# An attention stage issued in the order of a list plan, with wider products and four gates moved to the dense stage, in a one-core hybrid encoder block

## The chip, the cores and the metric

The kernel runs on 1 core of a Trainium2 chip. The core has five engines, each with its own queue of instructions: PE (TensorE, matrix products, with its weight loads listed apart as PEld), DVE (VectorE), ACT (ScalarE), POOL (GpSimd) and SP (SyncE, which here only issues transfers). [...] The metric is the device time of one execution in microseconds (us), lower is better.

## The reference

One layer of a streaming encoder, for 1024 frames of width 1024, in float32. A normed input goes through one combined projection, whose columns feed three token mixers and three gates. The mixers are a gated linear recurrence (HGRN, 4 heads of 128), forgetting attention (FoX, 8 heads of 64) and cross-attention into 256 memory tokens (4 heads of 128). Each mixer's result is projected, multiplied by its gate, and the sum is projected and added to the input; a convolutional GLU of width 2816 follows.

```python
h = _rmsnorm(x, norm_mix_g[l])
z = h @ w_in[l]
(hq, hf, hi, hg, fq, fk, fv, ff, mq, gate_logits) = jnp.split(z, pts, axis=-1)
y_a = _hgrn2_mixer(hq, hf, hi, hg, lower_bounds[l], hgrn_norm_g[l])
y_b = _fox_mixer(fq, fk, fv, ff, fox_f_bias[l], fox_q_norm_g[l], fox_k_norm_g[l])
...
y_c = _memory_mixer(mq, mem_kv, mem_q_norm_g[l], mem_k_norm_g[l])
gates = jax.nn.sigmoid(gate_logits).reshape(B, T, N_BRANCH, D_MODEL)
merged = (gates[:, :, 0] * (y_a @ w_br_hgrn[l]) + gates[:, :, 1] * (y_b @ w_br_fox[l])
          + gates[:, :, 2] * (y_c @ w_br_mem[l]))
x = x + merged @ w_out[l]
x = x + _conv_glu_ffn(_rmsnorm(x, norm_ffn_g[l]), ...)
```

The part that the change is about is FoX. For a block of 128 queries and all keys up to its end, per head:

```python
s = (jnp.einsum('bhqd,bhkd->bhqk', qh[:, :, lo:hi], kh[:, :, :hi]) * scale
     + Fc[:, :, lo:hi, None] - Fc[:, :, None, :hi])
p = jax.nn.softmax(jnp.where(mask, s, -jnp.inf), axis=-1)
outs.append(jnp.einsum('bhqk,bhkd->bhqd', p, vh[:, :, :hi]))
```

## The kernel before

**Number format.** A float32 operand is split (`split`, L172) into a high part, cast on ACT, and a low part, subtracted on DVE. One product block is then three matmuls, high by high, high by low and low by high (`mm3`, L158, lines L160 to L162 in the profile). Products go into four kinds of PSUM bank: `pp` (three), `lg` and `tr` (two each), `po` (one).

**Stages.** The kernel issues, in this order: the load and split of the input with the first gates; the *dense stage*, where pairs of 128-column chunks are projected at once by a fast scheme with seven block products in place of eight (`dense_unit`, L628, over `PAIRS`; the chunks are the four of the memory queries and `NPAIR` = 10 gates); the *memory stage* with cross-attention, beside the FoX values and the first q/k projection (L974); the *attention stage* (L980 to L985 and L1229 to L1235); the HGRN heads; the branches and the output projection; the feed-forward part, where both projections use the seven-product scheme again.

**Gates.** There are 24 chunks of gates. A gate that is not in the dense stage is projected alone by `gates_early` (L470) through `cm_chunk` (L200): for each half of the frames, eight `mm3` of 512 columns; DVE multiplies by the norm (L464), ACT applies tanh (L465) and SP sends the result to DRAM (`gd`), from where the branches fetch it. Ten of them are given to the attention stage, by `NFOX` = [0, 3, 0, 3, 0, 3, 1].

**Token-major projections.** `token_major` (L704) computes eight blocks of 128 frames by `ncol` channels, eight `mm3` each. `fox_proj(p)` (L844) makes q and k of head pair p, 256 columns, evacuated by ACT (L853) and normed (L859 to L862, with a POOL power at L179). `hgrn_values` (L1012) makes the HGRN values in two pieces of 256 columns, written straight into `Vf` over the FoX values. `fox_prep` (L866) transposes a pair's q and k by PE and splits them for the two heads on ACT, DVE and POOL.

**Attention.** `fox_attn(p, i)` (L901) works on one head. For each of eight query blocks, `rows`: scores in pieces of up to 512 keys (L924, L925), decay and running maximum by DVE (L930), exponent by ACT (L940), reciprocal by DVE (L941), normalising by POOL (L942). After each two blocks: transposes of the weights (L953, L954, L956), split by ACT and DVE, products with the values for 256 queries (L965, L966), and the sum of high and low parts (L969, L970) to DRAM (`ybd`).

**Order.** Python generators are woven together by `weave` (L97): a head's attention, at raised priority, with a token-major projection or with gates. The order of the instructions on each engine is then chosen by the framework's own scheduler, from these priorities and a model of time; `tc.issue_after` adds single edges. Weight blocks wait in three pairs of buffers, `wh` and `wl`.

```python
    for p in range(3):
        weave((ahead(fox_attn(p, 0), AHEAD), FOX_STEPS), (fox_proj(p + 1), 8))
        fox_prep(p + 1, fox_sets[p][3])
        weave((ahead(fox_attn(p, 1), AHEAD), FOX_STEPS), (gates_early(NFOX[2 * p + 1]), 2 * NFOX[2 * p + 1], FOX_LATE))
```

**After the attention.** `hgrn_prep(0)` projects the first HGRN head (six blocks, L1043). Before the memory branch its operands come back from DRAM by POOL transfers, all issued behind the last HGRN norm. In the feed-forward part `unit` (L1452) runs one seven-product unit; for the first of them `families` (L1495) makes the operand blocks, with two of the low parts of `B21` on POOL, and `spread` (L361) makes the norm's row.

Of the kernel before, what the change touches and what calls it, by code (L numbers as in the profile page):

```python
# [28 lines left out]
NCOVER, NPAIR = 2, 10  # L29
NDULL = 8  # L30
NFOX = [0, 3, 0, 3, 0, 3, 1]
# [3 lines left out]
assert 2 + NCOVER + NPAIR + sum(NFOX) == len(ORDER) and len(_dense) % 2 == 0  # L35
# [3 lines left out]
FOX_STEPS, HGRN_STEPS, MEM_STEPS = 28, 14, 7  # L39
AHEAD = 300  # L40
FOX_LATE = 0.2
# [66 lines left out]

@with_exitstack
def tile_block(ctx: ExitStack, tc: tile.TileContext, xT, memT, x_rows, mem_rows, vec, fbias, mats, hmask, w_first, w_cm, w_hi, w_fqk, w_fv,  # L110
# [77 lines left out]
    def weights(src, shape, raw=None, hl=None, parts=1):  # L188
# [4 lines left out]
        if hl is None:  # L193
            hl = [wp.tile([P, 4 * 264], F32R, tag=t, name=t, bufs=3) for t in ("wh", "wl")]
# [166 lines left out]
    def spread(r, rcol):  # L361

        for n in range(2):
            ps = ps_tr()
# [57 lines left out]
    def first_weights(k):  # L422
        k0, k1 = WFIRST[k]
        if k % 4 == 0:
            gw[k // 4] = [wp.tile([P, 4 * 264], F32R, tag=t, name=t, bufs=3) for t in ("wh", "wl")]
        sl = slice((k0 % 4) * 256, (k1 - 1) % 4 * 256 + 256)
        split(S, gw[k // 4][0][:, sl], gw[k // 4][1][:, sl], wg[k // 4][:, sl])
# [124 lines left out]
    def product(ps, op, b, first):  # L552
        wh, wl = op
        for k in range(4):
            ks = slice(k * P, (k + 1) * P)
            bh, bl = block(b, k)
            mm3(ps, wh[:, ks], wl[:, ks], bh, bl, first and k == 0, k == 3, not first)

    class Dense:
# [16 lines left out]
        def operand(self, src):  # L576
            if self.half is None:
                self.half = [wp.tile([P, 4 * 264], F32R, tag=t, name=t, bufs=3) for t in ("wh", "wl")]
# [125 lines left out]
    def token_major(src, ncol, evac):  # L704

        with tc.issue_after(late["load"].ins):
            w = [weights(src[q], (4, ncol)) for q in range(2)]
        for tb in range(8):
            ps = ps_proj()[:, :ncol]
            tsl = slice(tb * P, (tb + 1) * P)  # L710
            for k in range(KC):
                wh, wl = w[k // 4]
                mm3(ps, uh[k][:, tsl], ul[k][:, tsl], wh[:, k % 4, :], wl[:, k % 4, :], k == 0, k == KC - 1)
# [127 lines left out]
    fox_sets = {}  # L841
    fox_z = {}

    def fox_proj(p):  # L844

        fox_z[p] = [None, None]

        def evac(tb, ps):
            n, b = tb // 4, tb % 4
            if b == 0:  # L850
                fox_z[p][n] = pq.tile([P, 4, 256], F32, tag="z", name=f"z{p}_{n}", bufs=2)
            z = fox_z[p][n]
            S.activation(z[:, b, :], ps, AF.Copy, scale=rt[:, tb:tb + 1])  # L853
            if b == 3:
                zz = z.rearrange("p b (h d) -> p (b h) d", d=64)
                sq = pools["pf"].tile([P, 16, 64], F32, tag="pt", name="fsq", bufs=4) if p else \
                    pm.tile([P, 16, 64], F32, tag="fsq", name="fsq")
                r = cp.tile([P, 16], F32, tag="fr", name="fr", bufs=2)
                S.activation(sq, zz, AF.Square)  # L859
                V.reduce_sum(r, sq, axis=AX.X)  # L860
                rstd_small(r, r, 64)
                V.tensor_mul(zz, zz, r.unsqueeze(2).to_broadcast([P, 16, 64]))  # L862

        yield from token_major(w_fqk[p], 256, evac)

    def fox_prep(p, after=None):  # L866
        kh = [pf.tile([P, T], F32R, tag=f"kh{i}", name=f"kh{i}_{p}", bufs=1 + i) for i in range(2)]
        qa = [pf.tile([P, T], F32R, tag=f"qa{i}", name=f"qa{i}_{p}", bufs=1 + i) for i in range(2)]
        kl = [pf.tile([P, T], F32R, tag=f"kl{i}", name=f"kl{i}_{p}", bufs=1 + i) for i in range(2)]
        for n in range(2):  # L870
            sl = slice(n * HB, (n + 1) * HB)
            z = fox_z[p][n]
            for what in range(2):
                gc = col(C_FK) if what == 0 else fqs
                ptr = ps_tr()
                with tc.issue_after(after.ins) if after is not None else nullcontext():
                    for b in range(4):
                        PE.transpose(ptr[:, b * P:(b + 1) * P], z[:, b, what * P:(what + 1) * P], ident)
                for i in range(2):
# [935 lines left out]
```

## Time and profile before

| what | us |
|---|---|
| median of 3 runs | 1698.56 |
| lowest and highest run | 1698.53 and 1700.1 |
| the profiled execution, its own time | 1700.23 |
| its span, first to last instruction | 1698.4 |

The profile was taken from one execution, at a mean granted clock of PE of 0.999. In the lists of groups, a row gives the line, engine and operation, the tile written and those read, the shape and the count; then the busy time of the group and the mean duration of one; then the idle time of the engine in front of them and what ended it. In a table of stretches, each engine has its busy time and, behind x, the instructions that touch the stretch. The duration printed for a matmul is longer than the time until the next one starts, since they are pipelined; the pace of PE is read from starts or from counts. A transfer's row gives its queue, the count, the size and the median time from issue to landing.

### The profile page before, as it was taken

Reading aid. Unit: us, or ns where it says so; the run is one execution under the profiler, and the core shown is the slowest. Engines: PE = TensorE matmul, PEld = TensorE weight load, DVE = VectorE, ACT = ScalarE, POOL = GpSimd, SP = SyncE. Lnnn points to the kernel's source line nnn. Section 1 sums busy time; section 2 is a strip of 40 time slices with the busy share of each in tenths; the row PEclk is TensorE's granted clock in tenths of the full one; section 3 lists DMA queues with packets and bytes.
Section 4 is the critical chain, followed back from the end, with each engine's and each line's share of the span. In section 5 each row is a group of like instructions: output and inputs, shape, how many; then the busy total and the mean of one; then the engine's idle time right before and its main releaser. Section 6 shows DMA issues by size and latency. Waiting matters only on the chain.

```text
span 1698.4 us, 24291 instructions
## 1 busy us (share of the span) xinstructions
PE 1691.0 (100%) x8957; PEld 1452.4 (86%) x8957; DVE 1150.8 (68%) x2057; ACT 800.9 (47%) x1428; POOL 324.6 (19%) x420
## 2 busy tenths in 40 slices
PE   9999999999999999999999999999999999999999
PEld 7888899989898998888888888888888888888887
DVE  6966455666666664886856845987878888775654
ACT  6734455545454553775631333644434444533432
POOL 0200032543433331544310000311111111100000
PEclk9999999999999999999999999999999999999999
DMA  9443232221212111110346542566544344494772
GB/s 367 157 161 106 88 139 68 77 92 51 94 59 77 63 46 57 67 32 13 106 127 209 167 186 100 165 174 169 158 139 138 118 149 143 172 363 145 251 269 87
DMA packets 83062, 227.16 MB, mean 134 GB/s; under 512 B 9712, under 2 KB 12408, under 8 KB 82816
## 3 DMA queue, kind: packets, MB, share of 16 engines
q1 hardware_dynamic: 64320, 160.54, 26.8%
q0 software_dynamic: 18048, 64.50, 13.2%
q8 instruction: 70, 1.15, 0.3%
q10 hardware_dynamic: 576, 0.59, 0.1%
q14 instruction: 48, 0.39, 0.1%
HBM read 180.72 MB, written 67.93 MB: 146 GB/s over the span
## 4 chain that ended last, share of the span: by engine, by line
PE 99%; DVE 0%; ACT 0%; DMA 0%; issue 0%; ACTq 0%; DVEq 0%
PE pp L160 21%; PE pp L162 21%; PE pp L161 21%; PE lg L160 4%; PE lg L162 4%; PE lg L161 4%; PE tr L162 3%; PE tr L161 3%; PE tr L160 3%; PE po L966 1%; PE lg L925 1%; PE lg L924 1%; PE po L965 1%; PE po L160 1%; PE po L161 1%; PE po L162 1%
## 5 line engine op out<-in xcount | busy, mean ns | idle before, releaser
L160 PE MATMUL pp<-uh,wh 128*128 128x512 f32 x412 | 163.3, 396 | 0.0
L161 PE MATMUL pp<-ul,wh 128*128 128x512 f32 x412 | 162.9, 395 | 0.0
L162 PE MATMUL pp<-uh,wl 128*128 128x512 f32 x412 | 162.5, 394 | 0.0
L161 PE MATMUL pp<-wl,uh 128*128 128x256 f32 (+1 forms) x512 | 146.3, 286 | 0.0
L162 PE MATMUL pp<-wh,ul 128*128 128x256 f32 (+1 forms) x512 | 146.1, 286 | 0.0
L160 PE MATMUL pp<-wh,uh 128*128 128x256 f32 (+1 forms) x512 | 145.6, 286 | 0.0
L166 ACT CAST wh<-s 128x512 fp32r<-128x512 f32 x110 | 66.5, 621 | 131.6 <-PE pp L161 55.1
L166 ACT CAST wh<-raw 128x1024 fp32r<-128x1024 f32 (+2 forms) x76 | 67.6, 890 | 100.6 <-PE pp L161 86.2
L166 ACT CAST wh<-rw 128x512 fp32r<-128x512 f32 x87 | 53.2, 619 | 108.1 <-PE pp L161 70.2
L160 PEld LDWEIGHTS pp<-wh,uh 128*128 128x128 f32 x512 | 97.3, 190 | 1.2
L161 PEld LDWEIGHTS pp<-wl,uh 128*128 128x128 f32 x512 | 97.4, 190 | 1.0
L162 PEld LDWEIGHTS pp<-wh,ul 128*128 128x128 f32 x512 | 97.4, 190 | 0.9
L1457 POOL DMA_DIRECT2D rw<-in_w_up x44 | 24.1, 555 | 372.4 <-DVE wl L1350 171.3
L166 ACT CAST dwh<-wr 128x1024 fp32r<-128x1024 f32 (+1 forms) x41 | 40.2, 980 | 115.8 <-PE tr L161 40.0
L162 PEld LDWEIGHTS pp<-uh,wl 128*128 128x128 f32 x412 | 77.5, 188 | 15.1
L174 DVE TENSOR_TENSOR wl<-raw,wh 128x1024 fp32r<-128x1024 f32 (+2 forms) x75 | 78.0, 1040 | 17.8 <-ACT wh L166 17.6
L160 PEld LDWEIGHTS pp<-uh,wh 128*128 128x128 f32 x412 | 77.5, 188 | 14.6
L161 PEld LDWEIGHTS pp<-ul,wh 128*128 128x128 f32 x412 | 77.5, 188 | 14.5
L940 ACT ACTIVATE pt<-pt,st 128x128 f32<-128x128 f32 (+3 forms) x64 | 49.7, 777 | 41.7 <-DVE st L937 33.9
L174 DVE TENSOR_TENSOR dwl<-wr,dwh 128x1024 fp32r<-128x1024 f32 (+1 forms) x41 | 46.3, 1129 | 31.7 <-ACT dwh L166 31.7
L942 POOL TENSOR_SCALAR pt<-pt,st 128x128 f32<-128x128 f32 (+3 forms) x64 | 49.1, 767 | 78.4 <-DVE st L941 64.1
L1350 DVE TENSOR_TENSOR wl<-rw,wh 128x512 fp32r<-128x512 f32 x69 | 47.7, 704 | 22.7 <-PE pp L162 18.2
(500 smaller groups left out, 5123.2 us busy)
## 6 DMA issues: line engine op xcount, KB each, us to landing
rw<-in_w_up POOLq DMA_DIRECT2D x44, 512.0 KB, 4.7
sd<-in_w_dn POOLq DMA_DIRECT2D x30, 512.0 KB, 6.0
br<-yd SPq DMA_DIRECT2D x30, 512.0 KB, 5.0
raw<-in_w_cm SPq DMA_DIRECT2D x24, 512.0 KB, 3.4
gd<-gt SPq DMA_DIRECT2D x48, 256.0 KB, 2.0
gt<-gd SPq DMA_DIRECT2D x48, 256.0 KB, 2.7
yd<-fc SPq DMA_DIRECT2D x44, 256.0 KB, 2.2
wr<-sd SPq DMA_DIRECT2D x20, 512.0 KB, 4.5
```

What stands on the lines that cost most here:

```text
L160: PE.matmul(ps, lh, rh, start=first, stop=False, skip_group_check=more)
L161: PE.matmul(ps, lh, rl, start=False, stop=False, skip_group_check=more)
L162: return PE.matmul(ps, ll, rh, start=False, stop=last, skip_group_check=more)
L166: return S.copy(out, in_)
L174: return (sub or V).tensor_sub(l, src, h.bitcast(F32))
L924: PE.matmul(ps[:, :w], qa[i][:, tsl], kh[i][:, s0:s0 + w], start=True, stop=False)
L925: fox_sets[p][3] = PE.matmul(ps[:, :w], qa[i][:, tsl], kl[i][:, s0:s0 + w], start=False, stop=True)
L940: S.activation(pt[:, :ns], pt[:, :ns], AF.Exp, bias=st[:, 2:3], accum_out=st[:, 3:4])
L942: G.tensor_scalar(pt[:, :ns], pt[:, :ns], st[:, 3:4], 0.0, ALU.mult, ALU.add)
L965: PE.matmul(o, vhl[:, sb, :], ph[:, src], start=(sb == 0), stop=False)
L1350: late["split"] = V.tensor_sub(l, src, h.bitcast(F32))
L1457: late["raw"] = G.dma_start(raw[:, 2 * i:2 * i + 2, :], src[:, 2 * i:2 * i + 2, :])
```

## The change

Attention, its projections and its filler become *chains*: generators that yield an engine, a cost, and the earliest start, before they trace each instruction. `Plan.run` repeatedly takes the chain whose next step can start first (the lower rank at a tie), advances that engine's time and traces the step. `Plan.pin` adds to every instruction an order edge, without a semaphore, behind the one traced before it on its engine; so on all engines the order is that of the plan. `Ring` keeps the turn of rotating buffers. The costs are linear formulas. Steps of attention on PE get `SLACK` = 0.8 us on top of the time at which their inputs are ready.

Ranks: the chains of split and product after each transpose or score group 0, transposes of a head's weights 1, scores, values and decay rows 2, the pairs' q and k 3 (their evacuation 2), the later pairs' norm 4, weights 5, values back 6, filler 9. The filler, in order: the 256-column projection of pair 1; q and k of pairs 2 and 3 in one product of 512 columns (`w_late[0]`), sent to DRAM and fetched back per pair; six gates; the HGRN values in one product of 512 columns (`w_late[1]`), sent to DRAM and fetched into `Vf` when the last head's values are split. A head's weights are transposed and multiplied in two groups of four query blocks (512 queries).

Beside that: `NPAIR` is 14 in place of 10, so four gates move to the dense stage; `wh` and `wl` have four buffers; the first weights of HGRN are staged within the plan; the memory branch's operands are fetched two at a time behind gate loads of the first branch; in the opening of the feed-forward part a few steps change place or engine; and the store for POOL's transfer descriptors is set to 2048 bytes.

```diff
-NCOVER, NPAIR = 2, 10
+NCOVER, NPAIR = 2, 14
 NDULL = 8
...
-NFOX = [0, 3, 0, 3, 0, 3, 1]
+NFOX = 6
...
+SLACK = 0.8
+WIDE = 4
...
+    def pin(self):
+        traced = self.bb.bb.instructions
+        for i in traced[self.seen:]:
+            e = str(i.engine)
+            if e in self.last:
+                self.tc.add_manual_dep(i, self.last[e].name, mybir.DependencyInfo(
+                    mybir.DependencyClass.NoSync, mybir.DependencyReason.DATA), reason="order of the plan")
+            self.last[e] = i
+        self.seen = len(traced)
+
+    def run(self):
+        while self.chains:
+            self.chains.sort(key=lambda c: c[0])
+            for c in list(self.chains):
+                if callable(c[2]):
+                    t = c[2]()
+                    if t is not None:
+                        self.step(c, t)
+                        break
+            else:
+                best = min((c for c in self.chains if not callable(c[2])),
+                           key=lambda c: (max(c[2][2], self.free.get(c[2][0], 0.0)), c[0]))
+                eng, cost, ready = best[2]
+                start = max(ready, self.free.get(eng, 0.0))
+                self.free[eng] = start + cost
+                self.step(best, start)
...
+def pe_us(n):
+    return max(0.109, n * 0.000446)
+
+def act_us(n):
+    return 0.1 + 0.00082 * n
+
+def exp_us(n):
+    return 0.29 + 0.00084 * n
+
+def dve_us(n):
+    return 0.07 + 0.00105 * n
+
+def pool_us(n):
+    return 0.28 + 0.00083 * n
+
+
+PE_LAG, LAG = 0.25, 0.12
+LOAD, STORE = 4.0, 3.0
...
+    def rows():
+        for h in range(8):
+            p, i = divmod(h, 2)
+            t0 = yield lambda: max(qk_ready[p]) if len(qk_ready.get(p, ())) == 8 else None
...
+                    k, t = yield from lg.get()
                     ps = ps_lg()
-                    PE.matmul(ps[:, :w], qa[i][:, tsl], kh[i][:, s0:s0 + w], start=True, stop=False)
-                    fox_sets[p][3] = PE.matmul(ps[:, :w], qa[i][:, tsl], kl[i][:, s0:s0 + w], start=False, stop=True)
...
+                    t = yield "PE", 2 * pe_us(w), max(t, t0) + SLACK
+                    PE.matmul(ps[:, :w], qa[:, tsl], kh[:, s0:s0 + w], start=True, stop=False)
+                    PE.matmul(ps[:, :w], qa[:, tsl], kl[:, s0:s0 + w], start=False, stop=True)
+                    t += 2 * pe_us(w) + PE_LAG
+                    plan.add(0, reduced(row, s0, w, ps, k, max(t, tp, ts), nfm, kf, tf))
+            rows_done[h] = t
...
+    def outcomes():
+        for h in range(8):
+            tv = yield lambda: vh_ready.get(h)
+            for g in range(2):
+                pts = []
+                t0 = tv
+                for tb in range(4 * g, 4 * g + 4):
+                    yield lambda: (h, tb) in pt_ready or None
+                    pts.append(pt_ready[h, tb][0])
+                    t0 = max(t0, pt_ready[h, tb][1])
+                for sb in range(4 * g + 4):
+                    k, t = yield from tr.get()
+                    ptr = ps_tr()
+                    first = max(sb - 4 * g, 0)
+                    t = yield "PE", (4 - first) * pe_us(P), max(t, t0) + SLACK
+                    for j in range(first, 4):
+                        PE.transpose(ptr[:, j * P:(j + 1) * P], pts[j][:, sb * P:(sb + 1) * P], ident)
+                    t += (4 - first) * pe_us(P) + PE_LAG
+                    plan.add(0, outcome(h, g, sb, first, k, ptr, t))
+                pt_free[h, g] = t
+
+    def outcome(h, g, sb, first, k, ptr, t):
+        c = slice(first * P, HB)
+        w = HB - first * P
+        kp, tp = yield from pls.get()
+        ph = pf.tile([P, HB], F32R, tag="ph", name="ph", bufs=2)
+        pl = pf.tile([P, HB], F32R, tag="pl", name="pl", bufs=2)
+        t = yield "ACT", act_us(w), max(t, tp)
+        cast(S, ph[:, c], ptr[:, c])
+        t = yield "DVE", dve_us(w), t + act_us(w) + LAG
+        V.tensor_sub(pl[:, c], ptr[:, c], ph[:, c].bitcast(F32))
+        t += dve_us(w) + LAG
+        tr.free(k, t)
+        yield lambda: 0.0 if sb == 0 or turn.get((h, g)) == sb else None
+        if sb == 0:
+            ko, to = yield from po_ring.get()
+            kept[h, g] = ko, ps_po()
+            t = max(t, to)
+        ko, po = kept[h, g]
+        t = yield "PE", 2 * pe_us(w), t + SLACK
+        PE.matmul(po[:, c], vh[h][:, sb, :], ph[:, c], start=sb == 0, stop=False)
+        PE.matmul(po[:, c], vh[h][:, sb, :], pl[:, c], start=False, stop=sb == 4 * g + 3)
+        t += 2 * pe_us(w) + PE_LAG
+        turn[h, g] = sb + 1
...
+    def steps(j, per, w, mm, ready, last):
+        for q in range(KC):
+            hl, kw, tw = yield lambda: parts[j][q // per] if len(parts.get(j, ())) > q // per else None
+            t = yield "PE", 3 * pe_us(w), max(ready, tw)
+            mm(q, *hl)
+            if last and (q + 1) % per == 0:
+                ws.free(kw, t + 3 * pe_us(w))
+        return t + 3 * pe_us(w) + PE_LAG
+
+    def tokens(j, per, ncol, evac):
+        for tb in range(8):
+            k, t = yield from pp.get()
+            ps = ps_proj()[:, :ncol]
+            tsl = slice(tb * P, (tb + 1) * P)
+            t = yield from steps(j, per, ncol, lambda q, h, l: mm3(ps, uh[q][:, tsl], ul[q][:, tsl], h[:, q % per, :],
+                                                                  l[:, q % per, :], q == 0, q == KC - 1), t, tb == 7)
+            plan.add(1, evac(tb, ps, k, t))
+
...
+    def fill(gates):
+        yield from tokens(-1, 4, 256, pair_block)
+        for j in range(2 + len(gates)):
+            if j == 0 or j > len(gates):
+                yield from tokens(j, 2, HB, to_dram(zd, zd_ready) if j == 0 else to_dram(hid, hid_ready))
+                continue
+            for n in range(2):
+                k, t = yield from pp.get()
+                ps = ps_proj()
+                sl = slice(n * HB, (n + 1) * HB)
+                t = yield from steps(j, KC, HB, lambda q, h, l: mm3(ps, h[:, q, :], l[:, q, :], uh[q][:, sl], ul[q][:, sl],
+                                                                   q == 0, q == KC - 1), t, n == 1)
+                plan.add(1, gate_evac(gates[j - 1], n, ps, k, t))
+
...
+    def later_pairs():
+        for p in (2, 3):
+            cs = slice((p - 2) * 256, (p - 1) * 256)
+            for n in range(2):
+                t = 0.0
+                for tb in range(4 * n, 4 * n + 4):
+                    t = max(t, (yield lambda: zd_ready.get(tb)))
+                tz = (yield from zs.get())[1]
+                z = fox_tile(p, n)
+                t = yield "SP", 0.1, max(t, tz)
+                SP.dma_start(z, zd[4 * n:4 * n + 4, :, cs].rearrange("b p c -> p b c"))
+                plan.add(4, fox_norm(p, n, t + LOAD))
+
+    def values_back():
+        yield lambda: vh_ready.get(7)
+        for tb in range(8):
+            t = yield lambda: hid_ready.get(tb)
+            yield "SP", 0.1, max(t, vh_ready[7])
+            SP.dma_start(Vf[:, tb, :], hid[tb])
+
...
+    gates = list(islice(early, NFOX))
+    sources = [(w_late[0], (2, HB), 4)] + [(w_cm[16 + 8 * order[i][0] + order[i][1]], (KC, P), 1) for i in gates]
+    sources += [(w_late[1], (2, HB), 4), (w_cm[4], (KC, P), 1)]
+    zr.update({(0, 0): 0.0, (0, 1): 4.0})
+    plan = Plan(tc)
+    for rank, gen in ((2, rows()), (1, outcomes()), (3, pairs()), (2, value_parts()), (2, decays()), (5, stage_weights(sources)),
+                      (4, later_pairs()), (9, fill(gates)), (6, values_back())):
+        plan.add(rank, gen)
+    plan.run()
...
+    with tc.issue_after(plan.last[str(PE.engine)]):
+        run_all(hgrn_prep(0, parts[len(sources) - 1][0][0]))
...
+    for i, _ in enumerate(first_branch):
+        if i % 3 and i < 12:
+            p, c = i % 3 - 1, i // 3
+            mark = G.tensor_scalar(warm, late["gates"][:, 0:1], 1.0, 0.0, ALU.mult, ALU.add)
+            with tc.issue_after(mark.ins):
+                G.dma_start(yc[p][c], ycd[p][:, c, :].bitcast(F32R))
...
+        ins = product(y, o4, "B22", False)
+        if begun:
+            e2 = late["e2"]
+            with tc.issue_after(ins.ins):
+                spread(r2, rt2)
         put(0, 1, y, e2)
...
-                    late["last"] = family_block(name, k, quarters(k)[q], G if name == "B21" and k > 1 else None)
+                    late["last"] = family_block(name, k, quarters(k)[q])
+                    late["cast"] = late["split cast"]
...
-    nc = bacc.Bacc("TRN2", target_bir_lowering=False, num_devices=1)
+    nc = bacc.Bacc("TRN2", target_bir_lowering=False, num_devices=1, dynamic_dma_scratch_size=2048)
```

461 lines of the change are left out of this document (302 added, 159 removed).

## The prediction

> **What bounds the kernel now.** First the page, for which engine fills the span, and the chain of work that ended last.
>
> ```profile
> span 1698.4 us, 24291 instructions
> ## 1 busy us (share of the span) xinstructions
> PE 1691.0 (100%) x8957; PEld 1452.4 (86%) x8957; DVE 1150.8 (68%) x2057; ACT 800.9 (47%) x1428; POOL 324.6 (19%) x420
> ...
> PE 99%; DVE 0%; ACT 0%; DMA 0%; issue 0%; ACTq 0%; DVEq 0%
> ```
>
> The matrix engine is the chain: 99% of it. A change can only help by giving PE fewer or cheaper matmuls, and can only hurt by making PE wait. A busy PE isn't yet a PE at its own pace, so next I read stretches of time: one of weight loads against 256 columns, one of plain dense work, the attention stage (until the first HGRN head is projected), the HGRN stage, the opening of the feed-forward part, and the dense input stage.
>
> ```profile
> core 0: us, PE busy (x) PEld busy (x) DVE busy (x) ACT busy (x) POOL busy (x), PEclk, DMA share, GB/s
> 315.60:326.65 11.05, 11.05 (x95) 11.05 (x93) 7.95 (x10) 5.69 (x9) 7.15 (x6) 1.00 0.62 188
> 895.00:1065.00 170.00, 170.00 (x751) 140.56 (x750) 107.77 (x163) 54.07 (x77) 1.06 (x2) 1.00 0.46 161
> 325.00:690.00 365.00, 365.00 (x2395) 332.69 (x2394) 224.04 (x661) 186.36 (x362) 130.01 (x176) 1.00 0.20 66
> 690.00:895.00 205.00, 204.24 (x1183) 173.87 (x1182) 151.55 (x250) 122.68 (x298) 75.33 (x68) 1.00 0.22 71
> 50.00:212.00 162.00, 162.00 (x737) 134.70 (x736) 104.45 (x171) 76.61 (x133) 10.89 (x17) 1.00 0.35 126
> ...
> 1065.00:1090.00 25.00, 24.82 (x125) 20.66 (x125) 23.09 (x40) 16.94 (x33) 10.61 (x11) 1.00 0.55 160
> ```
>
> The 895 to 1065 us stretch holds only 512-column matmuls: 170.00 / 751 = 0.2264 us each, at a granted clock of 1.00. For the narrower ones the start times of the timeline serve, since the printed durations overlap.
>
> ```profile
> 407.05 0.38 PE L954 MATMUL tr<-ident,pt 128*128 128x128 f32 x2
> ...
> 407.48 0.38 PE L954 MATMUL tr<-ident,pt 128*128 128x128 f32 x2
> ...
> 408.17 0.28 PE L161 MATMUL pp<-wl,uh 128*128 128x256 f32 x1
> ...
> 410.08 0.28 PE L162 MATMUL pp<-wh,ul 128*128 128x256 f32 x1
> 410.20 0.22 PE L924 MATMUL lg<-kh,qa 128*128 128x128 f32 x1
> 410.26 0.28 PE L925 MATMUL lg<-kl,qa 128*128 128x128 f32 x1
> 410.37 0.33 PE L160 MATMUL pp<-wh,uh 128*128 128x256 f32 x1
> ```
>
> Seventeen 256-column matmuls start between 408.17 and 410.20, so 0.120 us each (the stretch from 315.60 us agrees: 11.05 / 92 whole ones = 0.120). A 128-column matmul of the split products takes (410.37 - 410.20) / 2 = 0.085, a transpose (407.48 - 407.05) / 4 = 0.108. For 384 columns I interpolate: 0.173. Now the groups of the attention stage, shapes kept apart.
>
> ```profile
> L160 PE MATMUL pp<-uh,wh 128*128 128x512 f32 x219 | 86.4, 394 | 0.0
> L161 PE MATMUL pp<-wl,uh 128*128 128x256 f32 x295 | 84.4, 287 | 0.0
> L966 PE MATMUL po<-pl,vhl 128*128 128x256 f32 x128 | 34.7, 293 | 0.0
> L953 PE MATMUL tr<-ident,pt 128*128 128x128 f32 x128 | 32.1, 276 | 0.0
> L924 PE MATMUL lg<-kh,qa 128*128 128x512 f32 x48 | 20.4, 425 | 0.0
> L966 PE MATMUL po<-pl,vhl 128*128 128x128 f32 x32 | 8.9, 278 | 0.0
> ```
>
> Each of the first two stands for three lines of its kind, some 655 and 884 matmuls. At the pitches above they are 655 x 0.2264 = 148.3 and 884 x 0.120 = 106.1 us; the products with the values (256 and 64) 36.2; the scores (96 of 512, 32 each of 384, 256 and 128, by the code) 33.8; the 344 transposes 37.2. That is 361.6 of 365.0 us. Only 3.4 us of this stage are lost, so a better order has almost nothing to win; what counts is the matmuls.
>
> **The change part by part.** *Four gates to the dense stage.* A gate projected alone is 2 x 8 x 3 = 48 matmuls of 512, so four leave 192. In the dense stage they form two more units of 7 products x 4 x 3 = 84, so 168 come in. 24 x 0.2264 = **5.4 us saved**. That stage has room for their evacuations: DVE is busy 104.45 of its 162.00 us, ACT 76.61.
>
> *Wide products.* The q/k projections of pairs 2 and 3 were 2 x 8 x 8 x 3 = 384 matmuls of 256 columns and become 192 of 512; so do the HGRN values. Each pair of narrow ones gives 2 x 0.120 - 0.2264 = 0.0136 us, and 192 of them 2.6 us; twice, **5.2 us saved**. [...]
>
> *Values by 512 queries.* A head now takes two groups of four query blocks in place of four groups of two. The columns are the same; 256 matmuls of 256 and 64 of 128 (36.2 us) become 96 of 512, 32 of 384, 32 of 256 and 32 of 128: 21.7 + 5.5 + 3.8 + 2.7 = 33.8. **2.4 us saved.** Scores and transposes keep their number.
>
> *New round trips.* Wide q/k blocks and the HGRN values go through DRAM and back, as the gates do already.
>
> ```profile
> gd<-gt SPq DMA_DIRECT2D x48, 256.0 KB, 2.0
> gt<-gd SPq DMA_DIRECT2D x48, 256.0 KB, 2.7
> raw<-in_w_fqk SPq DMA_DIRECT2D x8, 512.0 KB, 3.3
> ```
>
> Out and back is 2.0 + 2.7 = 4.7 us. It costs nothing while PE has filler: behind the last value block stand the first HGRN head's 144 projections, 144 x 0.2264 = 32.6 us, and behind the wide q/k blocks the gates. Without that cover it would be 4.7 us once for each of three hand-overs, 14 us. The DMAs add to a stage whose engines are busy 0.20 of the time. POOL's descriptor store shrinks from the default to 2048 bytes; nothing in the trace prices it. In this stage SP issues the transfers, so I take nothing, with the 4.7 us of one late load as the upper end and no gain, since a smaller store can't send sooner.
>
> *The order of the plan.* Every instruction of the stage is chained behind the one before it on its engine, in the order of a list schedule whose costs are formulas in the kernel; PE's attention steps are drawn 0.8 us later than their inputs, and projections fill in behind them. If an input is late, all that PE has behind it waits: filler, and through the PSUM banks ACT and DVE. The formulas against the rows:
>
> ```profile
> L174 DVE TENSOR_TENSOR pl<-tr,ph 128x512 fp32r<-128x512 f32 x48 | 32.2, 684 | 12.0 <-ACT ph L166 11.8
> L174 DVE TENSOR_TENSOR wl<-raw,wh 128x1024 fp32r<-128x1024 f32 x23 | 28.3, 1231 | 8.4 <-ACT wh L166 8.4
> L930 DVE CUSTOM_DVE_ANT_0 pt<-lg,nf 128x512 f32<-128x512 f32 x32 | 22.0, 689 | 20.8 <-PE lg L925 10.8 <-PE tr L953 9.7
> L464 DVE TENSOR_TENSOR gt<-pp,rx 128x512 f32<-128x512 f32 x20 | 13.8, 689 | 20.3 <-PE pp L162 20.3
> L862 DVE TENSOR_TENSOR z<-z,fr 128x1024 f32<-128x1024 f32 x6 | 9.1, 1509 | 0.7 <-POOL fr L179 0.7
> ```
>
> The plan has 0.608 for the first (0.684 measured), 1.145 for the second (1.231), 0.608 for a gate's multiply (0.689) and 1.145 for the last (1.509). So DVE is drawn 7 to 32% short by means, 0.08 us on the step from a transpose to its product, against 0.8 of reserve. I take the idle share of the HGRN stage, where PE's work is likewise small steps behind other engines: 0.76 of 205.00 us, on the new stage of 365 - 192 x 0.2264 - 5.2 - 2.4 = 314 us: **1.2 us lost**. Below, the order could at best win the 3.4 us. Above, it is bounded by a DVE that sets the pace (second case).
>
> *Opening of the feed-forward part.* One operand split and one PSUM copy move later, the spread of the norm goes behind the next product, and two subtractions move from POOL to DVE.
>
> ```profile
> 1082.36 0.39 PE L162 MATMUL tr<-B21h,wl 128*128 128x512 f32 x1
> 1082.93 0.50 PE L162 MATMUL pp<-B11h,wl 128*128 128x512 f32 x1 [0.18 <-DVE wl L1350]
> ```
>
> PE is 0.57 - 0.23 = 0.34 us late here, by DVE, which is busy 23.09 of 25.00 us. Two more subtractions of 0.68 are 1.4 us at worst; the later split could clear the 0.34. I take **0.3 lost**, between -0.3 and +1.4. The branch loads spread out behind gate loads, and the fourth weight buffer, move no matmul: nothing, covered by a PE with no idle time from 895 to 1065 us.
>
> Sum: -5.4 - 5.2 - 2.4 + 1.2 + 0.3 = **-11.5 us**. On the profiled execution, 1700.23 us with a span of 1698.4 and 1.8 around it, that is a span of 1686.9; it ran 1.7 above the median of 1698.56, so against the median **1687.1 us**.
>
> **The rivals.** *Attention outruns DVE (slower).* The plan gives filler the last rank, so attention is packed ahead and DVE is near full in that part. DVE has 224.04 us in the stage now; less 8 gate multiplies (5.5) and 4 gate splits (4.9) it is 213.6, and less what belongs to filler (12 multiplies 8.3, 19 splits 23.4) 182 for attention. If DVE takes 12% longer than drawn, within the 7 to 32% above, PE waits 21.8 us in place of 1.2: 1707.7. It turns slower than before from 12.7 us of waiting, 7%. For it: the means; a strict order can't swap in filler. [...] Against: the 0.8 us of reserve in front of every attention step of PE, and a DVE that on the stage's average is 213.6 / 314 = 68% busy.
>
> *Filler runs out.* It shrinks from 960 x 0.120 + 480 x 0.2264 = 224 to 192 x 0.120 + 672 x 0.2264 = 175 us. If the last head stands without it, PE does that head's (33.8 + 33.8 + 37.2) / 8 = 13 us in the 182 / 8 = 23 that DVE needs: 10 us idle, 1697. Against it: filler goes in only where attention isn't ready, and 175 us are more than half of the stage.
>
> *Nothing gained.* The plan's weights come late: 4 + 6 + 4 + 1 = 15 sets, each 3.3 us of landing and 1.2 of split. A wait of 0.8 us on each takes the 11.5 away: 1699. Against it: the fourth buffer loads one set further ahead.
>
> **How the numbers follow.** Forecast 0.62 (1687.1, own range 1682 to 1692: all 3.4 us won, or one late round trip lost), attention outruns DVE 0.18, filler runs out 0.12, nothing gained 0.08. A difference under 0.2%, 3.4 us, can't be told from no change here. Filler running out lands between the forecast and 1697, by how much of the head is bare; half of it, 0.06, I count as no difference. So faster 0.62 + 0.06 = 0.68, same 0.06 + 0.08 = 0.14, slower 0.18. The range runs from 1682 to 1703, inside the slow case, which leaves some 0.15 above and 0.05 below.
>
> **What would show it.** Right: 512-column matmuls still at 0.226 us; no 256-column group but one pair's and the first; an attention stage of some 314 us with PE idle under 4 us in it; a dense stage longer by 168 x 0.2264 = 38 us; DVE under 75% through the stage. Wrong: PE idle there that ends on DVE or ACT (the second case), idle only toward its end (filler), idle that ends on weights after a load. The prediction is wrong if PE idles over 5 us, or if the wide pitch is above 0.235.

## The result: slower by half a per cent

The changed kernel took 1707.85 us (median of six runs, 1705.07 to 1708.61), the kernel before 1698.68 beside it (six runs): a ratio of 1.0048, 95% interval 1.0035 to 1.0061. The forecast was 1687.1. The profiled execution of the changed kernel took 1705.88 us with a span of 1704.1, so it is one of the quicker ones. First its page, the same three lines as before.

```profile
span 1704.1 us, 23210 instructions
PE 1685.8 (99%) x8421; PEld 1422.6 (83%) x8421; DVE 1163.0 (68%) x2091; ACT 801.9 (47%) x1436; POOL 323.9 (19%) x428
...
PE 95%; DVE 3%; ACT 1%; issue 1%; DMA 0%; POOL 0%; ACTq 0%; POOLq 0%
```

536 matmuls are gone (8957 to 8421) and PE is busy 5.2 us less, yet the span is 5.7 us longer. The chain of waits, 99% PE before, now runs for 3% through DVE and 1% through ACT. Where that happens the windows tell: the dense input stage, the attention stage as a whole and in five parts, the HGRN stage, and the plain dense work behind it.

```profile
core 0: us, PE busy (x) PEld busy (x) DVE busy (x) ACT busy (x) POOL busy (x), PEclk, DMA share, GB/s
85.00:240.00 155.00, 155.00 (x686) 128.40 (x685) 91.23 (x144) 63.87 (x112) 6.41 (x12) 1.00 0.31 111
...
355.00:655.00 300.00, 290.03 (x1587) 246.97 (x1587) 211.43 (x647) 169.21 (x337) 130.88 (x177) 0.99 0.28 92
355.00:400.00 45.00, 39.75 (x275) 37.47 (x275) 33.83 (x94) 25.87 (x52) 27.01 (x32) 0.92 0.30 98
400.00:500.00 100.00, 99.80 (x528) 83.81 (x526) 75.89 (x231) 58.43 (x115) 52.50 (x68) 1.00 0.29 97
500.00:550.00 50.00, 47.27 (x250) 38.53 (x249) 40.56 (x122) 32.11 (x65) 23.92 (x35) 1.00 0.26 81
600.00:655.00 55.00, 53.21 (x276) 44.60 (x275) 28.70 (x93) 27.35 (x53) 12.62 (x20) 1.00 0.28 94
...
690.00:890.00 200.00, 200.00 (x1136) 169.44 (x1137) 132.27 (x228) 108.20 (x266) 64.67 (x55) 1.00 0.18 59
...
935.00:1065.00 130.00, 130.00 (x575) 107.73 (x574) 80.93 (x122) 46.80 (x65) 0.00 (x0) 1.00 0.39 138
```

In these stretches PE is idle for 10 us, all in the attention stage: 5.25 in its first 45 us, where the granted clock is 0.92 too, 2.7 between 500 and 550 us, 1.8 at the end. The dense stretches keep their pace (130.00 / 575 = 0.2261 us a matmul). The view of PE's waits between 340 and 690 us names what ended them; in the kernel before this view has no row between 300 and 705 us.

```profile
engine line waited for: us in total, times, longest us
PE tr L1034 <- DVE kl L1004: 5.2, 1, 5.2
PE po L1168 <- DVE pl L1157: 2.4, 4, 0.9
PE tr L1143 <- DVE qa L1004: 1.2, 2, 0.7
PE po L1167 <- ACT ph L254: 0.9, 1, 0.9
```

Idle time isn't all that is lost, because PE also runs at a lower clock (0.92 in the first 45 us) and, between small steps, behind its pitch (by up to 15.4 us in the HGRN stage of the kernel before, see the table). So I counted the matmuls between marks in both traces and set them at the pitches of the prediction ("work"); "over" is length less work.

```
us, from mark to mark                    before: length   work   over   after: length   work   over
to the first token-major q/k product             205.16                        242.90
to the first q/k transpose                       109.63  109.31   0.32         110.70  110.39   0.31
to the first HGRN score                          386.07  382.28   3.79         328.67  308.71  19.96
to the last HGRN transpose                       187.75  172.30  15.44         208.80  192.70  16.10
to the first product of the memory branch         42.94   42.71   0.23          44.08   43.84   0.24
to the feed-forward part                         136.00                        136.00
to the down projection                           423.09  422.21   0.88         424.43  422.21   2.22
to the last matmul                               203.77                        203.77
```

The work falls by 13.2 us (+37.7 + 1.1 - 73.6 + 20.4 + 1.1; some 20 us of projections now stand behind the first HGRN score). The time over it grows by 18.2, of which 16.2 are in the attention stage. The saving came; the order of the plan gave it back.

**The opening of the stage.** The timeline of PE in the changed kernel (start, duration; in brackets the idle time before it):

```profile
358.31 0.28 PE L250 MATMUL pp<-wh,ul 128*128 128x256 f32 x1
363.84 1.94 PE L1034 MATMUL tr<-ident,z 128*128 128x128 f32 x8 [5.25 <-DVE kl L1004]
...
365.79 0.42 PE L249 MATMUL pp<-wl,uh 128*128 128x256 f32 x1
366.00 0.41 PE L250 MATMUL pp<-wh,ul 128*128 128x256 f32 x1
```

After the 5.25 us of idling a 256-column matmul takes 0.21 us from start to start, not 0.120: the granted clock is 0.5 from 361.0 us for 6.83 us. PE idles until 363.84, so it works for 4.0 us of these and, if it does half as much in them, loses another 2.0. What the transposes wait for is in the timeline of the other engines.

```profile
354.24 0.68 ACT L1000 ACTIVATE kh<-tr,cv 64x512 fp32r<-64x512 f32 x1 [0.38 <-PE tr L1034]
354.88 2.90 POOL L267 TENSOR_TENSOR fr<-fr,mhalf 128x16 f32<-128x16 f32 x1 [10.44 <-DVE fr L266]
357.81 1.63 DVE L982 TENSOR_TENSOR z<-z,fr 128x1024 f32<-128x1024 f32 x1 [3.02 <-POOL fr L267]
359.36 2.11 DVE L1046 TENSOR_TENSOR vhl<-Vf,vhl 128x512 fp32r<-128x512 f32 x2
361.39 0.73 DVE L1004 SCALAR_TENSOR_TENSOR kl<-tr,cv,kh 64x512 fp32r<-64x512 f32 x1
362.16 0.68 ACT L1000 ACTIVATE kh<-tr,cv 64x512 fp32r<-64x512 f32 x1 [6.67 <-DVE kl L1004]
```

The low part kl could start when ACT's kh is done, at 354.9. But in the trace DVE keeps to the order of the plan, and kl starts at 361.39, behind the end of the norm of the second half (z at 357.81, itself waiting 3.02 us for POOL's 2.90) and two splits of values (from 359.36). The plan begins its clock with all engines free at 0 and that half ready at 4.0; the tail of the code before it isn't in it. The transposes bank stays full until kl and its like are through, and PE has been given the next transposes as its next step.

**Pair evacuations.** The waits view of all engines, 353 to 655 us, has these two rows.

```profile
ACT kh L1000 <- DVE kl L1004: 12.5, 7, 6.7
...
ACT qa L1000 <- DVE qa L1004: 6.2, 5, 2.2
```

The plan draws ACT's second copy beside DVE's first; on the chip ACT starts it only when DVE has ended (361.39 + 0.73, then 362.16). The two steps have only the PSUM bank in common, and not its partitions: 0 to 63 and 64 to 127. The wait here is read as one by the whole bank, since the code gives no other reason; the trace shows the wait (6.67 us ahead of 362.16) and not its reason. Whether it could be dropped was not tried.

**The end of the stage.** The last head's products wait too:

```profile
650.40 0.40 PE L250 MATMUL pp<-wh,ul 128*128 128x512 f32 x1
651.65 0.39 PE L1167 MATMUL po<-ph,vhl 128*128 128x256 f32 x1 [0.86 <-ACT ph L254]
652.97 0.38 PE L1168 MATMUL po<-pl,vhl 128*128 128x256 f32 x1 [0.93 <-DVE pl L1157]
```

### The profile page after: what moved, and what is told of

Same layout as the page of the kernel before. It is cut to its first block, busy times and chain, and to the rows that moved or that the text cites. A ratio compares the mean times of both kernels' runs of the same rounds, so it can differ in the third digit from the quotient of the medians.

```text
span 1704.1 us, 23210 instructions
## 1 busy us (share of the span) xinstructions
PE 1685.8 (99%) x8421; PEld 1422.6 (83%) x8421; DVE 1163.0 (68%) x2091; ACT 801.9 (47%) x1436; POOL 323.9 (19%) x428
## 4 chain that ended last, share of the span: by engine, by line
PE 95%; DVE 3%; ACT 1%; issue 1%; DMA 0%; POOL 0%; ACTq 0%; POOLq 0%
PE pp L248 20%; PE pp L250 20%; PE pp L249 20%; PE lg L248 5%; PE lg L250 5%; PE lg L249 5%; PE tr L249 3%; PE tr L248 3%; PE tr L250 3%; PE tr L1143 2%; PE po L1168 1%; PE po L248 1%; PE po L250 1%; PE po L249 1%; PE lg L1082 1%; PE lg L1081 1%
## 5 line engine op out<-in xcount | busy, mean ns | idle before, releaser
L250 PE MATMUL pp<-uh,wl 128*128 128x512 f32 x356 | 140.5, 395 | 0.0
L249 PE MATMUL pp<-ul,wh 128*128 128x512 f32 x356 | 140.5, 395 | 0.0
L248 PE MATMUL pp<-wh,uh 128*128 128x256 f32 (+2 forms) x384 | 126.2, 329 | 0.0
L249 PE MATMUL pp<-wl,uh 128*128 128x256 f32 (+2 forms) x384 | 124.1, 323 | 0.0
L250 PE MATMUL pp<-wh,ul 128*128 128x256 f32 (+2 forms) x384 | 123.8, 322 | 0.0
L250 PEld LDWEIGHTS pp<-wh,ul 128*128 128x128 f32 x384 | 73.3, 191 | 5.7
L248 PEld LDWEIGHTS pp<-wh,uh 128*128 128x128 f32 x384 | 73.5, 191 | 4.0
L249 PEld LDWEIGHTS pp<-wl,uh 128*128 128x128 f32 x384 | 73.6, 192 | 3.9
L1157 DVE TENSOR_TENSOR pl<-tr,ph 128x512 fp32r<-128x512 f32 (+1 forms) x96 | 50.6, 551 | 31.4 <-ACT ph L254 31.1
L254 ACT CAST ph<-tr 128x512 fp32r<-128x512 f32 (+1 forms) x96 | 42.9, 477 | 37.5 <-PE tr L1143 35.2
```

Source lines behind the costliest of these rows:

```text
L248: PE.matmul(ps, lh, rh, start=first, stop=False, skip_group_check=more)
L249: PE.matmul(ps, lh, rl, start=False, stop=False, skip_group_check=more)
L250: return PE.matmul(ps, ll, rh, start=False, stop=last, skip_group_check=more)
L254: return S.copy(out, in_)
L1157: V.tensor_sub(pl[:, c], ptr[:, c], ph[:, c].bitcast(F32))
```

## The experiments

The three places gave the first theories: the plan's opening, its pair evacuations, and a filler that doesn't last. Each run was timed against the kernel before on the same chip.

**e1_start: tell the plan when the engines are free.**

```diff
-    zr.update({(0, 0): 0.0, (0, 1): 4.0})
+    zr.update({(0, 0): 0.0, (0, 1): 6.8})
     plan = Plan(tc)
+    plan.free.update({"POOL": 5.0, "DVE": 6.6})
```

> The changed kernel, with one thing more: the plan starts with POOL taken for 5.0 us and DVE for 6.6 us, and counts the second half of pair 0 as ready at 6.8 us in place of 4.0, as the trace of the changed kernel shows them. The same instructions, in another order. Theory 'the plan starts from engines that are not free': the PE wait of 5.4 us at the start of the attention stage and the half clock behind it go, 1707.9 - 7 to - 9 = 1699 to 1701, and the granted clock is back near 0.999. Rival 'DVE is outrun': the wait comes back later in the stage, 1705 or more, with PE waits on DVE over 150 ns growing by 4 us or more. Rival 'the loss lies in the counts or outside the stage': no change.

1713.25 us, ratio 1.0075 [1.006, 1.009]: not a gain. The four largest of PE's waits:

```profile
PE tr L1143 <- POOL pt L1120: 5.5, 2, 3.0
PE tr L1143 <- DVE qa L1004: 3.9, 5, 1.0
PE po L1167 <- ACT ph L254: 1.7, 1, 1.7
PE tr L1034 <- DVE kl L1004: 1.6, 1, 1.6
```

The opening stall shrank from 5.2 to 1.6 us, but 5.5 and 1.7 us of waits came up at the end of the stage, with half clock for 6.8 us there, and the scattered ones grew.

**e2_pairs: draw a pair's four evacuations one behind the other.** One line at the end of the loop in `pair_evac`:

```diff
                 qk_ready.setdefault(p, []).append(end)
+            t = end
```

> The changed kernel, with the plan told that the four evacuations of a q/k bank run one behind the other (ACT, DVE, ACT, DVE), where it had ACT's second beside DVE's first; the trace shows ACT waiting for DVE there. Theory 'the plan draws what the chip doesn't do': the scattered waits on DVE rows kl, qa and pl between 470 and 550 us, 4.4 us, mostly go, and some of the wait at the start; 1702 to 1705. Rival 'DVE is outrun': the costs of DVE are the same, so the scattered waits stay, 1707 to 1708.

1710.18 us, 1.0056 [1.0041, 1.0071], where the theory had 1702 to 1705. The waits of the middle are gone, as it said; what is left are the opening (5.2) and one wait of 5.2 us for POOL's pt at 643 us, again at the end.

**e3_both: e1 and e2 together.**

> The edits of the last two together. Theory: the gains add, 1695 to 1698, PE idle under 5 us in the attention stage. Rival 'DVE is outrun': 1704 or more.

1705.74 us, 1.0033 [1.0019, 1.0048], some 8 us above the 1695 to 1698 of its theory. The first 45 us now are filled, and so is the middle; the end is emptier than in the changed kernel. Windows of e3_both:

```profile
355.00:400.00 45.00, 45.00 (x304) 41.56 (x304) 35.00 (x95) 26.41 (x51) 31.00 (x35) 1.00 0.31 108
500.00:550.00 50.00, 50.00 (x263) 42.12 (x262) 37.24 (x130) 30.40 (x61) 24.29 (x38) 1.00 0.30 98
600.00:655.00 55.00, 47.42 (x227) 38.11 (x226) 32.72 (x107) 27.69 (x54) 14.88 (x22) 0.88 0.31 98
```

So PE ran smoothly and spent its filler sooner, while attention took as long as ever: from the first q/k transpose to the last product with the values 298.8 us, against 299.7 in the changed kernel. The rest is idling (7.4 us) and half clock (13.65 us from 633.3). The opening and the pairs are real losses, but repairing them alone moves the loss to the end. The question became why attention takes 300 us, and whether it was the plan or the gates that are missing.

**e4_gates: the kernel before, with only the four gates moved.**

```diff
-NCOVER, NPAIR = 2, 10
+NCOVER, NPAIR = 2, 14
-NFOX = [0, 3, 0, 3, 0, 3, 1]
+NFOX = [0, 2, 0, 2, 0, 2, 0]
```

> The kernel before, with only the four gates moved to the dense stage (14 there, and two beside each of three heads in the attention stage). No plan, no wide products. Theory 'the counts save what they were forecast to save': 1698.7 - 5.4 = 1693.3. Rival 'the attention stage needs its filler': PE idles beside heads that have two gates in place of three, and 1697 or more.

1719.23 us, 1.011 [1.0095, 1.0125]. The edit that takes 24 matmuls away costs 18.8 us. Its waits between 300 and 705 us, where the kernel before has none, and the worst place in its timeline:

```profile
PE po L965 <- ACT ph L166: 3.5, 2, 2.9
PE lg L924 <- DVE st L930: 2.4, 5, 0.6
PE pp L160 <- DVE gt L1046: 2.2, 1, 2.2
PE po L966 <- DVE pl L174: 1.6, 3, 1.1
```

```profile
605.92 0.27 PE L954 MATMUL tr<-ident,pt 128*128 128x128 f32 x1
609.14 0.42 PE L965 MATMUL po<-ph,vhl 128*128 128x256 f32 x1 [2.94 <-ACT ph L166]
```

Counted as above, attention here takes 340 us, in which PE has 321 us of work; in the kernel before it takes 365 with 361. Without any plan, too, the gates had been what PE did while attention's other engines worked. By itself the move is a loss in this order.

**e5_ten: the changed kernel with ten gates kept in the stage** (`NPAIR` 10, `NFOX` 10).

> The changed kernel with the four gates back in the attention stage (NPAIR 10, NFOX 10 in place of 14 and 6); plan and wide products stay. Theory A, 'attention's own chain needs some 300 us and six gates are too little filler for it': PE then has 281 + 43.5 = 325 us of work in that stage, more than the chain, so the waits at its end and in its middle go; the one at the start (5.4 us and about 2 of half clock) stays. 1698.7 - 5.2 (wide) - 2.4 (values by 512) + 7.5 + 2 = 1700 to 1702. Theory B, 'the plan's order costs its waits whatever the filler': the waits stay and the 5.4 us of the dense scheme are lost, 1707.9 + 5.4 = 1713.

1709.88 us, 1.0061 [1.0048, 1.0075], some 8 us over the upper end of the forecast made for it. The waits at the end are gone, but the opening costs 5.3 us and half clock for 6.8, and other scattered waits 2.7: I had priced these two faults too low.

**e6_ten_both and e7_eight_both: e3 with ten and with eight gates** (`NPAIR` 10, `NFOX` 10; `NPAIR` 12, `NFOX` 8).

> The same, with both corrections of the plan's model (POOL taken for 5.0 us and DVE for 6.6 at the start; the four evacuations of a q/k bank one behind the other). Theory A: no PE wait of a microsecond in the stage, granted clock 0.999, 1698.7 - 7.6 + 1 to 2 = 1692 to 1693. Theory B: 1705.7 + 5.4 = 1711.

> The same two corrections, with eight gates in the attention stage (NPAIR 12, NFOX 8). Theory A: PE's work there is 281 + 21.8 = 303 us, about the 300 of attention's chain, so little waits: 1698.7 - 7.6 - 2.7 + 2 to 4 = 1690 to 1693. Theory B: 1705.7 + 2.7 = 1708.

1697.42 us, 0.9984 [0.9976, 0.9993], and 1694.99, 0.9975 [0.9965, 0.9985]. They lie 4 and 2 us above their forecasts, which start from 1698.7 for the kernel before; on this chip it took 1699.99. In neither does the view of PE's waits have a row for the stage; the window of e6_ten_both:

```profile
355.00:655.00 300.00, 300.00 (x1553) 253.37 (x1552) 193.53 (x591) 159.72 (x310) 108.96 (x152) 1.00 0.30 98
```

With the two faults mended and cover enough, the plan works, and e6 against e5 shows what the faults cost: 12.5 us. Attention still takes 303 us in both. It isn't the amount of filler that sets it.

**e8_slack: e3 with the reserve in front of PE's attention steps cut** (`SLACK` 0.8 to 0.2). In e3's timeline a turn of two blocks of transposed weights (256 and 128 queries) shows what the reserve does.

```profile
559.14 0.49 PE L1144 MATMUL tr<-ident,pt 128*128 128x128 f32 x3
...
559.55 0.61 ACT L254 CAST ph<-tr 128x256 fp32r<-128x256 f32 x2 [2.56 <-PE tr L1144]
...
559.96 0.62 DVE L1158 TENSOR_TENSOR pl<-tr,ph 128x256 fp32r<-128x256 f32 x2 [2.27 <-ACT ph L254]
...
561.55 0.28 PE L1168 MATMUL po<-ph,vhl 128*128 128x256 f32 x1
```

DVE has both low parts pl done at 560.58; the first of the four products that take them and their high parts ph begins 0.97 us later. With two transpose banks, two ph buffers and few pt buffers such a delay doesn't overlap away: it goes round with each turn.

> The two corrections, six gates, and the reserve in front of PE's attention steps at 0.2 us in place of 0.8. If the chain is long because each turn of it contains the reserve (12 transposes and their products for each of 8 heads, two banks: 96 x 0.6 / 2 = 29 us at most), attention ends 10 to 29 us earlier, the filler lasts and the time falls to 1690 to 1697. If the reserve keeps PE from waits for engines that run late, many waits of 0.2 to 0.6 us come up on DVE and ACT rows and the time stays at 1705 or rises. If it is an engine's throughput that sets the chain, no change, 1705.

1693.17 us, 0.9967 [0.9954, 0.998]: from one constant, 12.6 us under e3's median, or 12.1 by the distance of each from the kernel before on its own chip. Attention takes 278.7 us, and PE waits 0.4 us in all. Its waits, and then the window of the stage:

```profile
PE tr L1144 <- POOL pt L1121: 0.2, 1, 0.2
PE tr L1035 <- DVE qa L1004: 0.2, 1, 0.2
```

```profile
355.00:655.00 300.00, 299.52 (x1643) 256.98 (x1643) 215.71 (x653) 173.52 (x341) 137.15 (x181) 1.00 0.30 98
```

**e9_slack14, e10_slack_only, e11_four, e12_slack0: the size of it.** The reserve up, to 1.4, on e3; the reserve at 0.2 on the changed kernel with its two faults; e8 with two more gates moved (`NPAIR` 16, `NFOX` 4); e8 with no reserve.

> Both corrections of the plan's model, six gates, the reserve at 1.4 us. From 0.8 to 0.2 us the stretch from the first q/k transpose to the last product with the values fell from 298.8 to 278.7 us, 33.5 us for each us of reserve. Theory 'the reserve is in each turn of attention's chain, and the chain sets the length of the stage': 298.8 + 20 = 319 us, all of the addition as PE idle after the filler has run out, 1705.7 + 20 = 1726, a few us more for a halved clock. Rival 'an engine's throughput sets it': 299 us and 1706.

> The changed kernel with the reserve at 0.2 us and nothing else (none of the two corrections). If the reserve alone is the fault, as with the corrections: 1692 to 1695. If the errors of the plan's model cost by themselves, the wait at the start (5.4 us and some 2 of halved clock) stays and the waits on DVE rows kl, qa and pl grow, having less reserve: 1701 to 1706.

> Both corrections, the reserve at 0.2 us, and four gates in the attention stage in place of six (NPAIR 16). By the counts 2.7 us less than with six gates: 1690.5. By theory A (attention's chain of 279 us sets the stage, and with six gates PE's work up to its end is just as long) nothing is saved there, while the dense stage grows by 84 x 0.2264 = 19 us: 1693.2 + 19 - 4 (what filler was left behind the last head) = 1708, with PE idle behind the last filler.

> Both corrections, six gates, no reserve at all. The chain becomes some 272 us, shorter than PE's work, so nothing more is gained there: 1692 to 1694 if PE still finds its inputs ready. If the reserve is what kept PE from waiting, waits of 0.1 to 0.5 us come up at the 300 attention groups: 1696 or more.

e9: 1722.31 us, 1.0128 [1.0108, 1.0148]; PE waits at the end of the stage for every engine in turn.

```profile
PE tr L1144 <- POOL pt L1121: 5.3, 2, 3.4
PE lg L1082 <- DVE st L1096: 5.0, 4, 1.7
PE po L1168 <- DVE gt L1183: 3.2, 2, 1.6
```

e10: 1706.32, 1.0036 [1.0023, 1.0049]: the short reserve alone wins little, since the opening now costs 6.6 us and its half clock (6.8 us).

```profile
362.86 1.08 PE L1034 MATMUL tr<-ident,z 128*128 128x128 f32 x4 [6.63 <-DVE kl L1004]
```

e11: 1705.36, 1.0025 [1.0014, 1.0037], with runs from 1701.46 to 1707.98: by counts it should have gained 2.7 us on e8, and it lost 12. The end runs dry, 4.7 us for POOL's pt and 2.7 for pl. e12: 1695.41, 0.9970 [0.9959, 0.9981], between its two forecasts and not to be told from e8. In one table, from the traces: attention from first q/k transpose to last product with the values, the stage's work and the time over it (as above), PE's waits in it, and time at half clock.

```
run              reserve  gates   attention    work   over   waits   half clock   ratio
after              0.8      6       299.7     308.7   20.0     9.7       6.8      1.0048
e1_start           0.8      6       306       308.7   26.6    14.3       6.8      1.0075
e2_pairs           0.8      6       303       308.7   23.3    10.4      13.7      1.0056
e3_both            0.8      6       298.8     308.7   19.2     7.4      13.7      1.0033
e5_ten             0.8     10       301       352.2   18.0     8.0       6.8      1.0061
e6_ten_both        0.8     10       303.4     352.2    5.4     0         0        0.9984
e7_eight_both      0.8      8       302.7     330.5    5.4     0         0        0.9975
e9_slack14         1.4      6       313.9     308.0   35.0    15.9      23.9      1.0128
e10_slack_only     0.2      6       291.1     309.4   21.6    10.7       6.8      1.0036
e8_slack           0.2      6       278.7     309.4    6.4     0.4       0        0.9967
e11_four           0.2      4       280.7     287.7   22.0     9.4      10.2      1.0025
e12_slack0         0        6       275.5     309.8    8.4     1.2       0        0.9970
```

Each row but its ratio is one execution: e8's is the fastest of its five, e11's the slowest of its seven.

The length of attention follows the reserve (313.9, 298.8, 278.7, 275.5 on the mended plan), and hardly the gates (298.8, 302.7, 303.4 at 0.8; 278.7, 280.7 at 0.2). The time over the work is made of three parts. One is the waits. One I put at half of the time that PE works at the low clock (in e3 two 512-column matmuls start 0.43 us apart at 636.28, in place of 0.226); it is less than half of the column, because PE idles through part of it (2.0 us in the changed kernel, 4.5 in e3). The third is a rest of 5.4 to 6.0 us in e6, e7 and e8, which hardly wait, and of 7.2 to 11.6 in the others (before: 3.8); what it consists of isn't shown.

The stage's work holds 28.7 us of the first HGRN head's projections that stand behind attention's last product in the changed kernel. Without them PE has some 280 us of work with six gates, for 279 us of attention at a reserve of 0.2 (e8) and for 299 at 0.8 (e3). With four gates it has 259 for 281 (e11), with eight 302 for 303 (e7), with ten some 323 for 303 (e6). The mended plans that are 19 us or more short of work (e3, e9, e11) wait for 7 to 16 us in all; those that match it or have more wait for 1.2 or less. That is where the loss lies.

## Why the prediction was wrong

*Counts and pitches: right.* The three savings were put at 5.4 + 5.2 + 2.4 = 13.0 us; the work fell by 13.2. The dense stage grew by 37.7 us (38 foretold), wide matmuls run at 0.226 and narrow ones at 0.120 (2.28 us for the 19 from 356.03 to 358.31), as before. The three hand-overs through DRAM and the late weights cost PE nothing: no row of its waits names a weight or a DMA.

*The order of the plan: this is the step that failed.* It was 1.2 us, and measured 16.2. What the runs show in its place are two untrue inputs of the plan and a reserve that stretches attention beyond the cover that was left: with all three mended (e8) the time over the work is 6.4 us in place of 20.0. The 1.2 was the idle share of the HGRN stage, 0.76 of 205 us. That measure was too kind twice over. By matmuls at their pitches, the measure I had used for attention itself, the HGRN stage was already 15.4 us over its work (part of this may be my price for its small products). And a stage with other banks and another chain says nothing of a plan that begins with an untrue picture of the engines. Both inputs that were untrue stood in the code: all engines free at 0, and two evacuations of one bank drawn side by side. I checked the plan's durations (7 to 32% short) and not its dependences, which were the ones to cost.

*"Against 0.8 us of reserve": turned round.* The prediction counted the reserve as protection. It is a delay within each turn of attention's chain and makes the chain 20 us longer than 0.2 does (e3 to e8), long enough to outlast the filler.

*Filler runs out* (1697, chance 0.12) was the mechanism of the end, seen in e1, e2, e3, e9 and e11, and in small in the changed kernel. I set against it that 175 us of filler are more than half of the stage; the comparison that decides is PE's work against the length of attention's chain, 280 against 300. It was mis-sized as well because it counts the idle time of PE alone: in e3 13.65 us at half clock came with 7.4 us of waits.

*Attention outruns DVE* gave 1707.7, the time that came, but for another reason, so the match is luck: DVE is busy 211.43 of 300 us, 70%, and with no less to do (215.71) e8 has PE waiting 0.4 us. That the formulas draw DVE short isn't what cost the time. *Nothing gained* by late weights fell.

*Four gates to the dense stage* was priced as 24 matmuls saved, with the room in the dense stage named, and without a price for the cover that it takes from attention. In the kernel before that is 24 us (18.8 lost in place of 5.4 won, e4).

*Opening of the feed-forward part:* 0.3 foretold, 1.3 measured, inside its bounds. The wait is by DVE, as said; the timelines of the changed kernel and of e4_gates:

```profile
1087.90 0.50 PE L250 MATMUL pp<-B11h,wl 128*128 128x512 f32 x1 [1.49 <-DVE wl L1679]
```

```profile
1099.50 0.50 PE L162 MATMUL pp<-B11h,wl 128*128 128x512 f32 x1 [0.81 <-DVE wl L1350]
```

In e4, which has the old code here, this stretch is as long as in the changed kernel, with a wait of 0.36 us for DVE ahead of this one. So the edit isn't shown to be the cause; what else shifts it stays open.

Open as well are the 2 to 3 us that even the best plans (e6, e7, e8) have over their work more than the kernel before, and which of e1's numbers makes its scattered waits grow. Of the 13.0 us that were counted as saved, e8 keeps 6.8 (1693.17 against 1699.99).

## What to carry to other kernels

A planned order is worth as much as its picture of the chip: put in when each engine is really free and which steps run one behind the other in the trace, then read the trace for waits whose releaser had its own input long before. Keep a stage's side chain and PE's work in one sum: matmuls moved out of a stage are won only while PE's remaining work is longer than the chain, and past that point each costs several times what it saves (e4, e11). A safety margin inside a chain with few buffers is paid at every turn; where the order is right, a quarter of it served here (e8: 1693.17 us, faster than both kernels).

## What was not expected of the hardware

A stall cost more than its length. After 2.94 us of idling (e4) PE ran at a granted clock of 0.5 for 3.41 us, after 5.25 us (the changed kernel) for 6.83, and after 3.38 us followed by waits of 0.77 and 3.05 (e3) for 13.65: once, twice and four times 3.41. At that clock a 512-column matmul took 0.43 us from start to start (e3, 636.28 to 636.71) in place of 0.226, and a transpose 0.21 (the changed kernel, 364.29 to 364.50) in place of 0.108. So I put the loss at half of the time that PE works in such a stretch, here 1.6, 2.0 and 4.5 us.

Not every wait had such a stretch behind it. In the changed kernel waits of 0.22 to 0.73 us between 500 and 550 us, 0.86 and 0.93 at 651 us and 1.49 at 1087 us all passed at a granted clock of 1.00. In the 5.25 us of its opening the clock fell at 361.01, 2.4 us after PE's last matmul had ended; the ends of matmuls are modelled in a trace, so this is rough. In e3 the two later waits, 0.77 and 3.05 us, came while the clock was still low, and it stayed so for four times as long as in e4. What starts such a stretch and what ends it these runs don't show.
